# Partial sums of the fourth dense tile of a PEER layer leave PSUM every fourth block in place of every second

## The chip, the cores and the metric

The kernel runs on one core of a Trainium2 chip. The metric is the device time of one execution in microseconds (us), lower is better. Three runs of the kernel before gave 4597.64, 4600.57 and 4611.91 us; their median, 4600.57 us, is the time that a prediction is set against.

## The reference, cut to what matters

The program is a two-layer backbone over 256 context tokens and 512 latent tokens of width 1024. Each layer is a mixer (RWKV-7 heads and a Fourier transform in layer 0, attention and a convolution in layer 1) followed by a PEER layer, a product-key mixture of 16384 one-row experts. Only the PEER layer is touched:

```python
def chunk(tc):
    ...                                    # product keys: 16 experts per head and token, with a gate
    act = jax.nn.gelu(jnp.einsum("thkd,td->thk", pu[expert], tc), approximate=False) * gate
    return jnp.einsum("thk,thkd->td", act, pv[expert])
```

## The kernel before, in words

A PEER layer is computed in two ways side by side. **Dense tiles** (128 tokens each) are multiplied with all experts: the 16384 experts are 128 blocks of 128, and for a block `up_part` forms the activations of all dense tiles (matmuls of `proj`, line 392, into PSUM tile `pS`, then a Gelu on ScalarE, line 1237). They are multiplied by a table of gates that is zero for experts not chosen (line 1307, VectorE), and the products are contracted with the block's rows of `pv` (line 1291). **Gathered tiles** fetch their chosen rows of `pu` and `pv` one by one with an indirect DMA issued on GpSimd (line 1132), and VectorE reduces each row (lines 1137 and 1146). The fetches have three row buffers.

In layer 0 the four latent tiles are dense (`nd == 4`), and the two context tiles are gathered at the same time. In layer 1 three tiles are dense and one is gathered, and the lines that the change edits take the same values as before.

Every matmul runs three times, on high and low parts of its operands: `split` casts to the high part on ScalarE (line 379) and subtracts on VectorE for the low part (line 382). For block `it` of the down stage that gives four tiles, `ahi`, `alo` (activations) and `vhi`, `vlo` (rows of `pv`), the *part* of that block. They come from pools `act` and `pv`.

PSUM has eight banks. The sums of dense tiles 0 to 2 stay in six of them over all 128 blocks (`acc00` to `acc21`), and `pS` takes one. The fourth tile's sums, two halves of 512 columns, share the one that is left: PSUM tile `acc4` is filled from the last two parts for half 0, added to an SBUF tile of the same name by VectorE (line 1324; the very first time a ScalarE copy, line 1322), and then filled for half 1. So in every second block there are two groups of six matmuls (line 1320), and each may begin only when VectorE has emptied the bank after the group before. Four buffers of each part are there.

The order on each engine is set when the program is built, by a scheduler that plays the program through on its own timing; engines then run their lists strictly in order. `pace` hands out the gather steps over the blocks, so VectorE's list mixes casts, gate products, gather steps and the additions of line 1324. After the last block come the epilogue (lines 1352 and 1353, written out at line 1356) and the mixer of layer 1, which loads the two context tiles again (`nx`, line 207).

Of the kernel before, what the change touches and what calls it, by code (L numbers as in the profile page):

```python
# [17 lines left out]
PS = bass.MemoryType.PSUM  # L18
# [176 lines left out]
class Net:  # L195
# [1007 lines left out]
    def peer(self, l, dense, gath, xin, xout, front, done=None):  # L1203
# [5 lines left out]
        nd = len(dense)  # L1209
        n = nd * 128  # L1210
        with ExitStack() as st:
# [21 lines left out]
            def up_part(b, out, pS):  # L1233
                *u, i = self.wtile(up, self.I[f"l{l}_pu"][b], e_lo=V, q=nc.sync)
                p = pS.tile([128, 512], F32, name="pS")[:, :n]
                self.proj([(p, 0, n)], u, h)
                nc.scalar.activation(out=out, in_=p, func=AF.Gelu)  # L1237
                return i
            def pace(ins, w):
                nonlocal work  # L1240
                self.gstep(math.ceil(self.gleft * w / max(work, w, 1e-9)) if w else 0, ins)
                work -= w
            with ExitStack() as s2:
                sp, gp = self.tp(s2, "sel", 1), self.tp(s2, "gbig", 3)
                pp, pt = self.tp(s2, "gps", 3, space=PS), self.tp(s2, "gtp", 2, space=PS)
                pS = self.tp(s2, "pS", 2, space=PS)
# [14 lines left out]
            self.cs.close()  # L1261

            n3 = min(nd, 3)
            keep = 2 if nd == 4 else 1
            xp = self.tp(st, "act", 2 * keep)
            with ExitStack() as s2:
                pS = self.tp(s2, "pS", 3 - keep, space=PS)
                po = self.tp(s2, "acc", 1, space=PS)
                vw, gp = self.tp(s2, "pv", 2 * keep), self.tp(s2, "gl", 2)
                if nd == 4:  # L1270
                    acc4 = kp.tile([128, D], F32, name="acc4")
                parts = []
                acc = [[po.tile([128, 512], F32, name=f"acc{t}{hf}") for hf in range(2)] for t in range(n3)]

                pairs = sorted([((i + 0.5) / (NB // 2), 2 * i) for i in range(NB // 2)] +
                               [((i + 0.5 - OF) / (64 - NB // 2), NB + 2 * i) for i in range(64 - NB // 2)])
                order = [b + i for _, b in pairs for i in range(2)]
                fresh = [b for b in order if b >= NB]
                def go():
                    if fresh:  # L1280
                        b = fresh.pop(0)
                        ahead[b] = ap.tile([128, n], F32, name="a32f", bufs=2)
                        up_part(b, ahead[b], pS)
                ahead = {}
                go()
                def add(t, it, p):
                    ahi, alo, vhi, vlo = p
                    q = slice(t * 128, (t + 1) * 128)
                    for x, y, s, z in ((ahi, vhi, it == 0, False), (ahi, vlo, False, False), (alo, vhi, False, it == 127)):
                        for h2 in range(2):  # L1290
                            nc.tensor.matmul(acc[t][h2], x[:, q], y[:, h2 * 512:(h2 + 1) * 512], start=s, stop=z)  # L1291
                for it, b in enumerate(order):
                    if b % 2 == 0:
                        gt = gp.tile([128, 2 * nd, 2, 64], F32, name="gt")
                        nc.sync.dma_start(gt, gd[:, :, b:b + 2].rearrange("h p b t -> p h b t"))
                    vr = vw.tile([128, D], F32, name="vraw", bufs=2)
                    nc.sync.dma_start(vr, self.I[f"l{l}_pv"][b * 128:(b + 1) * 128])
                    vhi = vw.tile([128, D], F32R, name="vhi")
                    vlo = vw.tile([128, D], F32R, name="vlo")
                    self.split(vr, vhi, vlo)  # L1300
                    if b < NB:
                        a32 = ap.tile([128, n], F32, name="a32")
                        nc.sync.dma_start(a32, ad[b])
                    else:
                        a32 = ahead.pop(b)
                        go()
                    last = V.tensor_tensor(out=a32.rearrange("p (h t) -> p h t", t=64), in0=a32.rearrange("p (h t) -> p h t", t=64),  # L1307
                                           in1=gt[:, :, b % 2], op=OP.mult)
                    ahi = xp.tile([128, n], F32R, name="ahi")
                    alo = xp.tile([128, n], F32R, name="alo")  # L1310
                    self.split(a32, ahi, alo)
                    parts.append((ahi, alo, vhi, vlo))
                    four = nd == 4 and it % 2
                    for hf in range(2):
                        if four:
                            c = slice(hf * 512, (hf + 1) * 512)
                            p = po.tile([128, 512], F32, name="acc4")
                            for i, (xh, xl, yh, yl) in enumerate(parts):
                                for x, y, s, z in ((xh, yh, i == 0, False), (xh, yl, False, False), (xl, yh, False, i == 1)):
                                    nc.tensor.matmul(p, x[:, 384:512], y[:, c], start=s, stop=z)  # L1320
                            if it == 1:
                                nc.scalar.copy(out=acc4[:, c], in_=p)
                            else:
                                V.tensor_tensor(out=acc4[:, c], in0=p, in1=acc4[:, c], op=OP.add)
                        if it < 126 and hf == 0:
                            for t in range(n3):
                                add(t, it, parts[-1])
                    if it == 127:

                        for t in range(n3):  # L1330
                            for i in range(2):
                                add(t, 126 + i, parts[i - 2])
                    if four or nd < 4:
                        parts = parts[-1:] if nd < 4 else []
                    pace(last, W1 if b < NB else 2)
                self.gstep(self.gleft)
                if done:

                    done[0].close()
                    sp = self.tp(done[1], "ep", 2, side="right")  # L1340
                else:
                    sp = self.tp(s2, "ep", 2)
                xs = []
                for t in dense:
                    xs.append(sp.tile([128, D], F32, name="ex", bufs=nd))
                    self.load(xs[-1], xin[t])
                for i in ((3, 0, 1, 2) if nd == 4 else range(nd)):
                    x = xs[i]
                    for hf in range(2):
                        c = slice(hf * 512, (hf + 1) * 512)  # L1350
                        m = sp.tile([128, 512], F32, name="em")
                        V.tensor_tensor(out=m, in0=acc[i][hf] if i < 3 else acc4[:, c], in1=gr[:, c], op=OP.mult)
                        V.tensor_tensor(out=x[:, c], in0=x[:, c], in1=m, op=OP.add)
                    if l == 1:
                        self.final(x, sp)
                    nc.sync.dma_start(xout[dense[i]], x)
# [268 lines left out]
```

## Time and profile before

| what | value |
|---|---|
| median of three runs | 4600.57 us |
| the profiled execution's own time | 4596.4 us |
| its span on the core | 4594.3 us |
| TensorE matmul, busy | 4165.1 us (91%), 26113 matmuls |
| TensorE weight load, busy | 3437.0 us (75%) |
| VectorE, busy | 3539.4 us (77%) |
| ScalarE, busy | 1738.3 us (38%) |
| GpSimd, busy | 1614.0 us (35%) |
| mean granted TensorE clock | 0.945 |

The down stage of layer 0 lies between 1813 and 2922 us of the span (from the first matmul of line 1291 to the last of line 1320). Matmuls are pipelined: one is listed with some 0.39 us, and the next starts sooner than that, so that the number of matmuls in a stretch says more than the busy share. "PE" is TensorE's matmul, "PEld" its weight load, DVE is VectorE, ACT ScalarE, POOL GpSimd and SP the engine that issues most DMAs.

### The profile page before, as it was taken

To read this page: it belongs to the slowest core of one execution; us is meant where nothing else is said; L and a number is where in the kernel's file an instruction comes from. 1 tells how busy PE (TensorE), PEld (TensorE's weight loads), DVE (VectorE), ACT (ScalarE), POOL (GpSimd) and SP (SyncE) were. 2 spreads that over 40 slices of the span, in tenths; PEclk is the share of its full clock that TensorE was granted. 3 is DMA by queue.
4 is the path that set the end of the run, shared out by engine and by line. 5 is a ranking of instruction groups with operands and counts; after the bars stand their busy time and mean duration, and the time that the engine had idled before them with its cause. 6 is when DMAs were issued, how large, how long until landed. Compare 5 with 4: busy or idle time off the path is not lost. (4 is left out here: it accounts for less than half of the span.)

```text
span 4594.3 us, 69774 instructions
## 1 busy us (share of the span) xinstructions
PE 4165.1 (91%) x26113; PEld 3437.0 (75%) x26113; DVE 3539.4 (77%) x6647; ACT 1738.3 (38%) x2847; POOL 1614.0 (35%) x1146
## 2 busy tenths in 40 slices
PE   7998899984777998999999999879999979999998
PEld 5775668872656887777778888666789968888887
DVE  2676667798898997888787887685489968788875
ACT  3443123332213665222222222336437733333333
POOL 1432212315642231444444444383220034444430
PEclk9998899995888999999999999989999989999999
DMA  4344884336777788889898988411236599999994
GB/s 170 92 108 102 264 297 125 119 106 203 228 236 234 271 309 293 302 309 320 295 320 309 309 304 290 145 32 33 71 105 215 217 345 336 340 330 339 344 333 145
DMA packets 487280, 1062.00 MB, mean 231 GB/s; under 512 B 95095, under 2 KB 265847, under 8 KB 477207
## 3 DMA queue, kind: packets, MB, share of 16 engines
q1 hardware_dynamic: 371740, 594.02, 39.2%
q0 software_dynamic: 110592, 402.70, 25.2%
q10 hardware_dynamic: 4608, 60.82, 3.3%
q8 instruction: 206, 3.38, 0.3%
q14 instruction: 134, 1.09, 0.1%
HBM read 927.83 MB, written 129.56 MB: 230 GB/s over the span
## 5 line engine op out<-in xcount | busy, mean ns | idle before, releaser
L1132 POOL DMA_INDIRECT row<-in_l_pv_dram,gi x384 | 563.3, 1467 | 837.0 <-DVE rows L1146 706.3
L1132 POOL DMA_INDIRECT row<-in_l_pur_dram,gi x384 | 490.3, 1277 | 953.8 <-DVE ga L1137 532.6
L392 PE MATMUL pS<-h2hi,whi 128*128 128x512 f32 (+1 forms) x2048 | 757.0, 370 | 35.3 <-ACT a L1237 29.6
L392 PE MATMUL pS<-h2hi,wlo 128*128 128x512 f32 (+1 forms) x2048 | 754.7, 369 | 7.8 <-DVE wlo L382 7.8
L392 PE MATMUL pS<-h2lo,whi 128*128 128x512 f32 (+1 forms) x2048 | 753.4, 368 | 0.0
L1137 DVE CUSTOM_DVE_ANT_0 row<-row,rows 128x1024 f32<-128x1024 f32 x384 | 498.7, 1305 | 185.0 <-DMA row<-in_l_pur_dram,gi 183.0
L379 ACT CAST whi<-wraw 128x1024 fp32r<-128x1024 f32 x327 | 344.3, 1054 | 759.4 <-PE pS L392 554.9
L1146 DVE SCALAR_TENSOR_TENSOR rows<-row,ga,rows 128x1024 f32<-128x1024 f32 x381 | 488.5, 1282 | 148.5 <-DMA row<-in_l_pv_dram,gi 146.3
L1291 PE MATMUL acc<-vhi,ahi 128*128 128x512 f32 x1536 | 469.7, 392 | 14.8 <-ACT ahi L379 14.8
L1291 PE MATMUL acc<-vlo,ahi 128*128 128x512 f32 x1536 | 479.6, 391 | 0.8 <-DVE vlo L382 0.8
L1291 PE MATMUL acc<-vhi,alo 128*128 128x512 f32 x1536 | 471.3, 391 | 1.5 <-DVE alo L382 1.4
L392 PEld LDWEIGHTS pS<-h2hi,whi 128*128 128x128 f32 x2048 | 391.0, 191 | 83.4 <-ACT a L1237 31.8
L392 PEld LDWEIGHTS pS<-h2hi,wlo 128*128 128x128 f32 x2048 | 390.3, 191 | 50.9 <-DVE wlo L382 9.2
L392 PEld LDWEIGHTS pS<-h2lo,whi 128*128 128x128 f32 x2048 | 390.4, 191 | 43.8
L382 DVE TENSOR_TENSOR wlo<-wraw,whi 128x1024 fp32r<-128x1024 f32 x266 | 324.3, 1220 | 71.0 <-ACT whi L379 70.9
L379 ACT CAST vhi<-vraw 128x1024 fp32r<-128x1024 f32 x256 | 264.8, 1050 | 206.7 <-PE acc L1291 117.7
L1291 PEld LDWEIGHTS acc<-vhi,ahi 128*128 128x128 f32 x1536 | 288.3, 189 | 69.2 <-ACT ahi L379 15.2
L382 DVE TENSOR_TENSOR vlo<-vraw,vhi 128x1024 fp32r<-128x1024 f32 x256 | 309.8, 1221 | 37.1 <-ACT vhi L379 36.9
L1291 PEld LDWEIGHTS acc<-vlo,ahi 128*128 128x128 f32 x1536 | 289.4, 189 | 63.0 <-DVE vlo L382 1.5
L1291 PEld LDWEIGHTS acc<-vhi,alo 128*128 128x128 f32 x1536 | 288.9, 188 | 63.7 <-DVE alo L382 2.8
L379 ACT CAST ahi<-a32f 128x384 fp32r<-128x384 f32 (+1 forms) x148 | 83.3, 563 | 570.2 <-DVE a32f L1307 274.0
L1120 ACT ACTIVATE gbig<-gps 128x256 f32<-128x256 f32 x448 | 232.4, 670 | 112.1 <-PE gps L1118 86.8
(460 smaller groups left out, 7950.0 us busy)
## 6 DMA issues: line engine op xcount, KB each, us to landing
wraw<-in_l_pu_dram SPq DMA_DIRECT2D x256, 512.0 KB
vraw<-in_l_pv_dram SPq DMA_DIRECT2D x256, 512.0 KB
gd<-gbig ACTq DMA_DIRECT2D x28, 2048.0 KB
mw<-in_l_mod_w_dram SPq DMA_DIRECT2D x48, 1024.0 KB
gt<-gd SPq DMA_DIRECT2D x64, 512.0 KB
wraw<-in_l_pq_dram SPq DMA_DIRECT2D x48, 512.0 KB
gt<-gd SPq DMA_DIRECT2D x64, 384.0 KB
ab<-arb SPq DMA_DIRECT2D x24, 768.0 KB
```

The source lines that it names most:

```text
L379: e.copy(out=hi, in_=src)
L382: return (e_lo or nc.vector).tensor_tensor(out=lo, in0=src, in1=hi.bitcast(F32), op=OP.subtract)
L392: nc.tensor.matmul(ps, a[:, k, :], b[:, k, t0:t0 + n], start=s, stop=e)
L1120: nc.scalar.mul(out=g[:, :, t0 - h0:t0 - h0 + 4].rearrange("p e t -> p t e"), in_=p[:, :, i * 64:i * 64 + 64], mul=1.0 / GSC)
L1132: nc.gpsimd.indirect_dma_start(out=r, out_offset=None, in_=self.I[f"l{l}_{src}"], in_offset=bass.IndirectOffsetOnAxis(ap=idx[:, s:s + 1], ...
L1137: V.tensor_tensor_reduce(out=r, in0=r, in1=acc, scale=1.0, scalar=0.0, op0=OP.mult, op1=OP.add, accum_out=act[:, s:s + 1])
L1146: V.scalar_tensor_tensor(out=acc, in0=r, scalar=act[:, s:s + 1], in1=acc, op0=OP.mult, op1=OP.add)
L1291: nc.tensor.matmul(acc[t][h2], x[:, q], y[:, h2 * 512:(h2 + 1) * 512], start=s, stop=z)
```

## The change

The fourth tile's groups are formed in every fourth block, from the last four parts: twelve matmuls per group instead of six, half as many groups, and so half as many additions from PSUM into SBUF (62 of line 1324 where there were 126; the two copies of line 1322 remain). A part has to live up to four blocks now, so each of `ahi`, `alo`, `vhi` and `vlo` gets six buffers instead of four. These take 24 KB more of each partition. The buffers of `pS` (one with four dense tiles, two otherwise) and all of layer 1 keep their numbers.

```diff
-            keep = 2 if nd == 4 else 1
-            xp = self.tp(st, "act", 2 * keep)
+            xp = self.tp(st, "act", 6 if nd == 4 else 2)
             with ExitStack() as s2:
-                pS = self.tp(s2, "pS", 3 - keep, space=PS)
+                pS = self.tp(s2, "pS", 1 if nd == 4 else 2, space=PS)
                 po = self.tp(s2, "acc", 1, space=PS)
-                vw, gp = self.tp(s2, "pv", 2 * keep), self.tp(s2, "gl", 2)
+                vw, gp = self.tp(s2, "pv", 6 if nd == 4 else 2), self.tp(s2, "gl", 2)
...
-                    four = nd == 4 and it % 2
+                    four = nd == 4 and it % 4 == 3
...
-                                for x, y, s, z in ((xh, yh, i == 0, False), (xh, yl, False, False), (xl, yh, False, i == 1)):
+                                for x, y, s, z in ((xh, yh, i == 0, False), (xh, yl, False, False), (xl, yh, False, i == 3)):
...
-                            if it == 1:
+                            if it == 3:
```

With one line less, line 1291 becomes 1290, 1320 becomes 1319, 1324 becomes 1323, and so on. The scheduler orders the whole stage anew. TensorE's list has the same matmuls. A group of the second half of the columns, early in the stage, before and then with the change (each row writes `acc4` from one part; the number behind a name counts buffers handed out):

```order
L1291 MATMUL acc01_17629<-vlo_18409,ahi_18415 128x512
L1320 MATMUL acc4_18344<-vhi_18199,ahi_18237 128x512
L1320 MATMUL acc4_18344<-vlo_18200,ahi_18237 128x512
L1320 MATMUL acc4_18344<-vhi_18199,alo_18238 128x512
L1320 MATMUL acc4_18344<-vhi_18276,ahi_18314 128x512
L1320 MATMUL acc4_18344<-vlo_18277,ahi_18314 128x512
L1320 MATMUL acc4_18344<-vhi_18276,alo_18315 128x512
L1291 MATMUL acc00_17628<-vhi_18408,alo_18416 128x512
```

```order
L1319 MATMUL acc4_18427<-vhi_18191,ahi_18229 128x512
L1319 MATMUL acc4_18427<-vlo_18192,ahi_18229 128x512
L1319 MATMUL acc4_18427<-vhi_18191,alo_18230 128x512
L1319 MATMUL acc4_18427<-vhi_18268,ahi_18306 128x512
L1319 MATMUL acc4_18427<-vlo_18269,ahi_18306 128x512
L1319 MATMUL acc4_18427<-vhi_18268,alo_18307 128x512
L1319 MATMUL acc4_18427<-vhi_18347,ahi_18354 128x512
L1319 MATMUL acc4_18427<-vlo_18348,ahi_18354 128x512
L1319 MATMUL acc4_18427<-vhi_18347,alo_18355 128x512
L1319 MATMUL acc4_18427<-vhi_18384,ahi_18391 128x512
L1319 MATMUL acc4_18427<-vlo_18385,ahi_18391 128x512
L1319 MATMUL acc4_18427<-vhi_18384,alo_18392 128x512
```

Two groups of six become one of twelve. In the list before, 16 to 42 other matmuls stand between the end of a group and the start of the next (none before the very last group). With the change 23 to 37 stand there in 48 of the 63 places and 68 to 73 in the other 15.

On VectorE, from the addition of one half to that of the other, early in the stage (`rows` is the gathered tile's sum, one row of it per gather step; `acc` stands for `acc4`), before and then with the change:

```order
L1324 TENSOR_TENSOR acc_17627<-acc_18318,acc_17627 128x512
L1307 TENSOR_TENSOR a_18639<-a_18639,gt 128x512
L1307 TENSOR_TENSOR a_18676<-a_18676,gt 128x512
L1146 SCALAR_TENSOR_TENSOR rows_6122<-row,ga_7655,rows_6122 128x1024 x3
L382 TENSOR_TENSOR alo<-a32f,ahi 128x512
L1324 TENSOR_TENSOR acc_17627<-acc_18344,acc_17627 128x512
```

```order
L1323 TENSOR_TENSOR acc_17627<-acc_18395,acc_17627 128x512
L1146 SCALAR_TENSOR_TENSOR rows_6122<-row,ga_7655,rows_6122 128x1024 x3
L382 TENSOR_TENSOR vlo<-vraw,vhi 128x1024
L1146 SCALAR_TENSOR_TENSOR rows_6122<-row,ga_7655,rows_6122 128x1024
L1323 TENSOR_TENSOR acc_17627<-acc_18427,acc_17627 128x512
```

The gather steps, 350 in the stage in both, stand among the rest much as they did: 32 times three or more of them follow each other before, 31 times with the change. In 20 of the 31 batches the second addition stands right behind a `vlo`, in 3 of all 126 additions before.

On the queue of SP, where layer 0 ends and the mixer of layer 1 begins (`x_5_101` is the epilogue's first tile written out, `nx` the reloaded context tiles), before and then with the change:

```order
L207 DMA dw<-in_dw_w_dram 128x62
L207 DMA nx<-x_0_96 128x1024
L207 DMA nx<-x_1_97 128x1024
L1356 DMA x_5_101<-ex 128x1024
L1356 DMA x_3_99<-ex 128x1024
```

```order
L207 DMA dw<-in_dw_w_dram 128x62
L1355 DMA x_5_101<-ex 128x1024
L207 DMA nx<-x_0_96 128x1024
L207 DMA nx<-x_1_97 128x1024
L1355 DMA x_3_99<-ex 128x1024
```

The two loads moved behind the first write of the epilogue. In layer 1 rows of all engines but GpSimd change places here and there; what is computed there is the same.

## Rows read from the trace of the kernel before

**Rows 1.** Busy time by stretch: from:to, us, engines, granted clock, DMA share, GB/s.

```profile
1813.00:2922.00 1109.00, 1073.12 (x4637) 872.71 (x4635) 882.00 (x1060) 299.66 (x393) 469.35 (x349) 0.99 0.88 302
1900.00:2500.00 600.00, 567.69 (x2415) 456.56 (x2414) 478.67 (x631) 156.72 (x204) 260.55 (x200) 0.98 0.89 309
2500.00:2900.00 400.00, 399.29 (x1759) 329.53 (x1758) 321.66 (x340) 110.60 (x145) 165.80 (x121) 1.00 0.87 295
2600.00:2700.00 100.00, 100.00 (x443) 82.81 (x442) 80.08 (x85) 29.73 (x39) 44.20 (x31) 1.00 0.90 306
```

**Rows 2.** TensorE's waits, 1900 to 2500: us in total, times, longest.

```profile
PE acc L1320 <- DVE acc L1324: 28.3, 24, 2.7
PE acc L1320 <- DVE alo L382: 2.4, 2, 1.2
...
PEld acc L1320 <- DVE acc L1324: 41.3, 33, 3.1
```

**Rows 3.** VectorE's waits, 1900 to 2500, the longest in total.

```profile
DVE row L1137 <- DMA row<-in_l_pur_dram,gi: 73.4, 53, 3.8
DVE rows L1146 <- DMA row<-in_l_pv_dram,gi: 36.6, 26, 4.2
```

**Rows 4.** VectorE by line, 1900 to 2500: count, busy us, mean ns, idle before.

```profile
L1137 DVE CUSTOM_DVE_ANT_0 row<-row,rows 128x1024 f32<-128x1024 f32 x128 | 155.2, 1222 | 73.9 <-DMA row<-in_l_pur_dram,gi 73.4 <-issue 0.2
L1146 DVE SCALAR_TENSOR_TENSOR rows<-row,ga,rows 128x1024 f32<-128x1024 f32 x72 | 92.4, 1284 | 37.1 <-DMA row<-in_l_pv_dram,gi 36.6
L1324 DVE TENSOR_TENSOR acc<-acc,acc 128x512 f32<-128x512 f32 x66 | 45.2, 684 | 0.0
```

**Rows 5.** Timeline of VectorE: start, us, instruction, idle before it and what ended it.

```profile
2208.10 1.23 DVE L1137 CUSTOM_DVE_ANT_0 row<-row,rows 128x1024 f32<-128x1024 f32 x1 [3.76 <-DMA row<-in_l_pur_dram,gi]
...
2209.76 1.23 DVE L1137 CUSTOM_DVE_ANT_0 row<-row,rows 128x1024 f32<-128x1024 f32 x1 [0.42 <-DMA row<-in_l_pur_dram,gi]
...
2210.91 0.69 DVE L382 TENSOR_TENSOR alo<-a32f,ahi 128x512 fp32r<-128x512 f32 x1
2211.51 0.69 DVE L1324 TENSOR_TENSOR acc<-acc,acc 128x512 f32<-128x512 f32 x1
```

**Rows 6.** TensorE at the same place: its timeline, then the stretch that follows.

```profile
2209.16 0.39 PE L392 MATMUL pS<-h2hi,whi 128*128 128x512 f32 x1
2212.25 0.50 PE L1320 MATMUL acc<-vhi,ahi 128*128 128x512 f32 x1 [2.71 <-DVE acc L1324]
...
2212.00:2218.00 6.00, 5.75 (x18) 4.59 (x19) 6.00 (x10) 0.18 (x1) 3.06 (x3) 0.72 0.90 300
```

**Rows 7.** GpSimd's longest waits, 1900 to 2500.

```profile
POOL row L1132 <- DVE ga L1137: 198.8, 101, 4.7
POOL row L1132 <- DVE rows L1146: 105.5, 52, 7.8
```

**Rows 8.** Timeline at the stage's end: SP, ACT, DVE and PE.

```profile
2900.18 0.93 SPq L207 DMA_DIRECT2D nx<-x  x2
2924.09 7.77 SPq L1356 DMA_DIRECT2D x<-ex  x4
...
2906.78 1.06 ACT L310 ACTIVATE nj<-nx 128x1024 f32<-128x1024 f32 x1 [6.48 <-DMA nx<-x]
...
2909.76 0.75 DVE L314 TENSOR_SCALAR nj<-nx,ns 128x1024 f32<-128x1024 f32 x1
2921.45 0.69 DVE L1324 TENSOR_TENSOR acc<-acc,acc 128x512 f32<-128x512 f32 x1 [0.30 <-PE acc L1320]
2930.83 0.69 DVE L1353 TENSOR_TENSOR ex<-ex,em 128x512 f32<-128x512 f32 x1
...
2919.75 0.50 PE L1320 MATMUL acc<-vhi,ahi 128*128 128x512 f32 x1 [0.78 <-DVE acc L1324]
```

**Rows 9.** Layer 1's PEER stage: its stretch, and TensorE's longest wait, 3700 to 4594.

```profile
3800.00:4500.00 700.00, 699.46 (x3421) 621.64 (x3420) 563.60 (x699) 249.45 (x340) 308.40 (x222) 1.00 0.95 336
...
PE acc L1291 <- ACT ahi L379: 14.8, 1, 14.8
```

## The prediction

> **What bounds the kernel now.** I first asked which part of the program the change can reach at all: the down stage of layer 0, 1813 to 2922 us, which has every matmul of line 1320. The table of stretches comes first. Where TensorE waits for nothing it starts 443 matmuls in 100 us, one per 0.2257 us [rows 1]. At that pace the 2415 matmuls between 1900 and 2500 us need 545 us and take 600: 55 us are lost. The 1759 matmuls between 2500 and 2900 need 397 us and take 400. So nearly all that can be won in this stage lies in those 600 us.
>
> The list of TensorE's waits says what ends them. 24 times the engine stood idle until line 1324 had emptied `acc4`, 28.3 us in all; the weight loads, which come a step earlier, met the same wait 33 times [rows 2]. Idle time counts from the end of a 0.39 us matmul, though the next could have started 0.226 us after its start, so each wait costs 0.16 us more: 28.3 + 24 x 0.16 = 32 us. The granted clock is the second loss. In the 6 us after one such wait it is 0.72 on average, the lower level (1.2 GHz) for part of them, after 2.71 us of idling [rows 6]; over the 600 us it is 0.98 [rows 1], which is 600 x 0.02 = 12 us. Together 44 of the 55 us hang on the additions; the rest is small waits for `alo` and what I can't assign.
>
> Then I asked why the additions are late. VectorE's waits in the same stretch are for gathered rows: 73.4 and 36.6 us [rows 3], 110 of the 121 us in which it idles (600 less 478.7 [rows 1]). None of its long waits is for TensorE. The timeline shows it in one place: VectorE waits 3.76 us for a row, reduces it and another, does an `alo`, and only then the addition, and TensorE starts 2.71 us late [rows 5, 6]. GpSimd in turn waits for VectorE to give a row buffer back [rows 7]. So here **VectorE's list, with the fetches it waits for, is the slower chain**, and TensorE meets it at line 1324.
>
> **The change part by part.** *Half the additions go.* 66 of them stand in the stretch, 0.684 us each [rows 4]; 33 remain, and 33 x 0.684 = 22.6 us leave VectorE's list. I work out what that is worth in two ways.
>
> From TensorE: 66 meetings become 33, and 7 of these have 68 or more matmuls (15 us at 0.2257) between the groups, against waits of at most 3.1 us [rows 2] that came with at most 42 (9.5 us); those can't wait. 26 of 66 remain, so 44 x 40/66 = 27 us are saved, if VectorE's list gets shorter by as much.
>
> From VectorE: since its list is the slower chain, the stretch gets shorter by what leaves it, 22.6 us, less what its waits for rows grow by. Where the row behind a removed addition is late anyway, VectorE only waits longer. 79 of the stretch's 200 gather steps wait (53 + 26 [rows 3], 128 + 72 [rows 4]); if the addition ahead of every such step were lost in its wait, 40% of 22.6 would go and 13.6 us be left. But most of a fetch's cycle starts when VectorE hands a buffer back [rows 7], so a step that comes earlier also fetches earlier, and the gather steps stand in runs of the same length as before. I take 21 us, close to the upper end, and keep 13.6 and 27 as bounds.
>
> The Trainium skill (Perfetto Trace Analysis, Identifying the Most-Contended Engine) judges TensorE by the busy share of its weight loads rather than of its matmuls, and other engines by occupancy. By that rule VectorE is the more contended in the stretch (80% against 76%) and TensorE in the next (82% against 80%) [rows 1], which agrees with where the loss is; by matmul busy share (95%) TensorE would be it in both, and the sum would be TensorE's 27 us.
>
> *The rest of the stage.* Between 2500 and 2900 us TensorE runs at its pace [rows 1]; additions that go there free VectorE and buy nothing. TensorE's matmuls are the same in number and shape. The four-part group starts as late as its last part, as the two-part group did.
>
> *Two more buffers of each part* take a cause of waiting away and add none: a part lives longer, but when a group ends four buffers come free and two parts are still ready, as before. What it could cost is bunching, since four casts become possible at once; that is a rival below. Zero, while the casts hide beneath the 36 matmuls of line 1291 (8 us) that two ready blocks give TensorE.
>
> *The end of the stage.* Before, the last addition comes after the last matmul, and TensorE waits 0.78 us just ahead of that [rows 8]. Now 13 matmuls follow the last group, 2.9 us, which cover a 0.69 us addition. Gain 1.5 us.
>
> *The reloads of the context tiles* move behind the epilogue's first write on SP, which waits for VectorE's epilogue. Before, they were issued at 2900.18, ScalarE began with them at 2906.78 and VectorE scaled the first at 2909.76 [rows 8], all beneath the last matmuls. Now they go out where the write did, at 2924.1 or 1.5 earlier. With the same 6.6 and 3.0 us the first is ready at about 2932, the epilogue on VectorE ends at 2931.5 (2930.83 + 0.69 [rows 8]), and two scalings (0.75 us each) with their reciprocals come on top. With the queue emptier than before the load may be faster; with the writes of the other tiles in its way, slower. Loss 2.5 us, 0 to 6.
>
> *Layer 1* does the same work in a slightly different order. From 3800 to 4500 us TensorE never stops there (3421 matmuls, clock 1.00); its one long wait is 14.8 us [rows 9]. I take 0, and half that wait, 7 us, either way as bounds.
>
> Sum against the profiled execution's own 4596.4 us: -21 - 1.5 + 2.5 + 0 = -20, 4576.4 us. The median of the runs is 4.2 us above that execution, so I forecast 4600.6 - 20 = 4580.6 us.
>
> **The rivals.**
>
> *A, TensorE comes close to its pace.* If the additions are also what holds the gather back (GpSimd waits for VectorE 304 us of the stretch [rows 7]), rows come earlier, and most of the 55 us return, say 40: 4600.6 - 40 = 4560. For it: TensorE and VectorE each wait for the other's chain now, so a shorter one helps twice. Against: VectorE's list would have to get 40 us shorter, 17 more than leave it.
>
> *B, the rows take it.* VectorE waits for rows as much longer as it has less to do. The fetches run beside matmul operands on a DMA that is 0.89 busy [rows 1], and a faster stage asks for more. Then 5 us or so remain: 4596.
>
> *C, bunched casts, and slower.* In 20 of 31 batches the second addition stands right behind a `vlo`, whose buffer the group before it has to free, and ScalarE must cast ahead of it. If that holds VectorE up once per batch ahead of a gather step, GpSimd gets its buffer late and the next row waits as well: 73.4/53 = 1.4 us per wait [rows 3], times 32 batches is 45 us, against 22.6 saved: +22, 4623. It decides from 0.7 us per batch (22.6/32). Against: 23 to 37 matmuls, 5.2 us and more, lie between two groups, and rows are bunched as before.
>
> *D, given back in layer 1.* The stage gains, and another wait like the one of 14.8 us [rows 9] arises in layer 1's new order: 4595.
>
> **How the numbers follow.** Chances: the forecast 0.50 (its own range 4566 to 4594, from the bounds 13.6 and 27 and the two ends of the smaller terms), A 0.15, B 0.18, C 0.09, D 0.08. A measurement of this kernel can tell about 0.3%, 13.8 us, from no change: faster means below 4586.8, slower above 4614.4. Of the forecast 0.45 lies below and 0.05 within; with A faster is 0.60. The rest of the forecast, B and D make 0.31 within, and C 0.09 slower. The range runs from 4556 (A and a little beyond) to 4603 (past B and D); C and the far side of A are left out.
>
> **What the trace of the changed kernel would show.** Right: 62 additions of 0.68 us; the idle time that they end on TensorE down from 28.3 us to some 12 between 1900 and 2500 (that is, in the blocks that stood there), with a higher granted clock; VectorE's waits for rows about as long as now; the stage some 21 us shorter; the first matmul of layer 1's projections 1 us later after the last one of the stage. Wrong: waits for rows that grow by 10 us or more (B); TensorE waiting as long as now with half the additions, or for `vlo` and `alo` (C); a stage of under 1075 us (A); a layer 1 whose length changes by more than 7 us (D). My argument fails as a whole if VectorE turns out to wait for TensorE in the stretch, since then its list was not the slower chain.

## The result and the profile after

The changed kernel is slower. Four runs of it gave 4655.74, 4638.55, 4656.03 and 4659.77 us, median 4655.89; four runs of the kernel before on the same chip gave a median of 4599.10. The ratio is 1.0104, with a 95% interval of 1.0083 to 1.0124, so some 48 us by the ratio and 57 by the medians. Forecast were 4580.6 us, faster than before, and a range of 4556 to 4603; the time lies 53 us above that range.

The profiled execution took 4655.74 us, its span 4654.0, its mean granted clock 0.939 (0.945 before). Lines of the changed kernel are numbered one lower than before: 1290 for 1291, 1319 for 1320, 1323 for 1324. The down stage of layer 0 now lies between 1816 and 2979 us. Its table of stretches (columns as in [rows 1]: stretch, its length, the busy time of TensorE matmul, weight load, VectorE, ScalarE and GpSimd with counts, granted clock, DMA share, GB/s):

```profile
1816.00:2979.00 1163.00, 1086.99 (x4636) 881.78 (x4634) 845.45 (x995) 297.22 (x385) 445.73 (x349) 0.98 0.84 287
1900.00:2500.00 600.00, 550.18 (x2317) 442.80 (x2316) 441.82 (x574) 151.00 (x195) 250.65 (x194) 0.97 0.86 297
2500.00:2900.00 400.00, 380.10 (x1642) 310.67 (x1641) 288.98 (x298) 105.69 (x137) 134.40 (x116) 0.98 0.85 282
```

Against [rows 1] the stage is 54 us longer with the same matmuls, and VectorE has 37 us less to do in it (845 against 882). The loss is in both parts: 98 matmuls fewer between 1900 and 2500 us (22 us at 0.2257 us each), and 117 fewer (26 us) between 2500 and 2900, where TensorE had run at its pace. The program ahead of the stage took 3 us longer. What follows the stage took 1675.0 us (4654.0 less 2979), against 1672.3 before.

The waits of the whole stage (total us, times, longest):

```profile
ACT vhi L379 <- DMA vraw<-in_l_pv_dram: 259.4, 56, 11.6
...
ACT vhi L379 <- PE acc L1319: 130.2, 15, 12.4
DVE rows L1146 <- DMA row<-in_l_pv_dram,gi: 127.3, 83, 3.9
...
DVE row L1137 <- DMA row<-in_l_pur_dram,gi: 85.5, 55, 3.8
DVE vlo L382 <- ACT vhi L379: 56.0, 23, 6.7
...
PE acc L1319 <- DVE acc L1323: 40.5, 18, 5.6
...
PE pS L392 <- ACT a32f L1237: 15.5, 6, 4.0
...
PE acc L1290 <- ACT ahi L379: 7.6, 5, 2.1
PE acc L1319 <- ACT ahi L379: 7.5, 3, 4.0
```

The same list before:

```profile
DVE rows L1146 <- DMA row<-in_l_pv_dram,gi: 97.2, 72, 4.6
...
PE acc L1320 <- DVE acc L1324: 31.1, 27, 2.7
...
ACT vhi L379 <- DMA vraw<-in_l_pv_dram: 10.4, 7, 3.0
```

The first line stands out. `vraw` is the buffer into which a block's rows of `pv` are loaded; ScalarE casts it to `vhi`, VectorE subtracts for `vlo`, and then the buffer is free. There are two of them, in both kernels. ScalarE waited for them 10.4 us before and 259.4 us after. VectorE never waited for `vhi` before; now it does so 23 times. Its waits for rows grew from 170.6 us (73.4 of [rows 3] and 97.2) to 212.8. TensorE's meetings with the addition became fewer (18 in place of 27) and longer.

On TensorE two waits are new, both for work of ScalarE: 15.5 us until the Gelu of line 1237 has emptied `pS`, and 15.1 us for `ahi`. One of them, by the timelines of ScalarE and TensorE:

```profile
2545.85 2.00 ACT L379 CAST vhi<-vraw 128x1024 fp32r<-128x1024 f32 x2 [8.23 <-PE acc L1319]
2558.01 1.04 ACT L379 CAST vhi<-vraw 128x1024 fp32r<-128x1024 f32 x1 [10.16 <-DMA vraw<-in_l_pv_dram]
...
2559.90 0.59 ACT L1237 ACTIVATE a32f<-pS 128x512 f32<-128x512 f32 x1
...
2560.54 0.79 PE L392 MATMUL pS<-h2hi,whi 128*128 128x512 f32 x1 [3.84 <-ACT a32f L1237]
```

ScalarE stood 10.16 us for a raw block, the Gelu behind it in its list came late (no idle time stands ahead of it), and TensorE stood 3.84 us for the Gelu. Over the stage TensorE's idle time grew from 36 us (1109 less 1073.1) to 76 (1163 less 1087.0), and its granted clock fell from 0.99 to 0.98, an estimated 12 us more (1163 x 0.02 less 1109 x 0.01); together that is about the 54 us.

One batch of four, by ScalarE's timeline (start, duration, instruction, idle before it and what ended it):

```profile
2219.46 2.00 ACT L379 CAST vhi<-vraw 128x1024 fp32r<-128x1024 f32 x2
2229.36 1.05 ACT L379 CAST vhi<-vraw 128x1024 fp32r<-128x1024 f32 x1 [7.90 <-DMA vraw<-in_l_pv_dram]
2231.90 1.05 ACT L379 CAST vhi<-vraw 128x1024 fp32r<-128x1024 f32 x1 [1.50 <-DMA vraw<-in_l_pv_dram]
```

and by SP's, which issues the loads:

```profile
2196.25 2.13 SPq L1296 DMA_DIRECT2D vraw<-in_l_pv_dram  x2
...
2224.13 12.09 SPq L1296 DMA_DIRECT2D vraw<-in_l_pv_dram  x4
```

Two raw blocks had been asked for at 2196 and lay ready until TensorE's second group, from 2217.17 on, read four parts for the last time and freed them within 3 us:

```profile
2217.17 0.50 PE L1319 MATMUL acc<-vhi,ahi 128*128 128x512 f32 x1 [2.52 <-DVE acc L1323]
...
2219.79 0.39 PE L1319 MATMUL acc<-vhi,alo 128*128 128x512 f32 x1
```

Two casts followed directly. The third block could be asked for only at 2224.13, when the first `vlo` had given a raw buffer back, and ScalarE stood for 7.90 us. The group itself had begun 2.52 us late, behind the addition of the first half.

### The profile page after: what moved, and what is told of

The parts are those of the page before. It is cut to its first block, busy times and chain, and to the rows that moved or that the text cites. A ratio compares the mean times of both kernels' runs of the same rounds, so it can differ in the third digit from the quotient of the medians.

```text
span 4654.0 us, 69618 instructions
## 1 busy us (share of the span) xinstructions
PE 4186.2 (90%) x26113; PEld 3451.8 (74%) x26113; DVE 3498.6 (75%) x6583; ACT 1739.2 (37%) x2847; POOL 1593.1 (34%) x1146
## 5 line engine op out<-in xcount | busy, mean ns | idle before, releaser
L1132 POOL DMA_INDIRECT row<-in_l_pv_dram,gi x384 | 536.3, 1397 | 902.8 <-DVE rows L1146 765.7
```

The costliest lines, as they stand in the source:

```text
L1132: nc.gpsimd.indirect_dma_start(out=r, out_offset=None, in_=self.I[f"l{l}_{src}"], in_offset=bass.IndirectOffsetOnAxis(ap=idx[:, s:s + 1], ...
```

## The experiments

The comparisons are ratios to the kernel before, run beside each kernel on the same chip. Two causes were suspected: the raw buffers, for the loss, and the rows, for the gain that didn't come.

### More raw buffers

```diff
-                    vr = vw.tile([128, D], F32, name="vraw", bufs=2)
+                    vr = vw.tile([128, D], F32, name="vraw", bufs=3)
```

The second run has 4 there, and `bufs=5` for `alo`.

> The changed kernel with three buffers of the raw value block (vraw) in place of two. Theory R (raw ring): four part buffers come free together, four casts want four raw blocks, two buffers hold two, and the third load is issued only after the first second-part subtraction; ScalarE's wait for raw blocks, 259 us in the stage of the changed kernel against 10 before, falls to between 100 and 180 us, and the time to 4605 to 4635. Rival H (parts held): four of six part buffers are held until the group, and two ahead are too few whatever feeds them: the time stays within 10 us of 4656, and ScalarE's wait only moves from raw blocks to part buffers. Rival S (the second half's group waits for the first half's addition, which has one accumulator between them): the time stays within 10 us of 4656 and TensorE's waits of 40.5 us for additions stay.

> The changed kernel with four buffers of the raw value block; for their space one of the six buffers of the activations' second part (alo) is given up. Theory R: as many raw blocks wait as parts come free: ScalarE's wait for raw blocks falls below 80 us in the stage, VectorE's waits for casts (56 us) below 20, and the time to 4570 to 4605. Rival H: within 10 us of 4656 or above it, since one buffer fewer makes it worse. Rival S: within 10 us of 4656.

Three raw buffers gave 1.0045 (1.0028 to 1.0062), four 1.0038 (1.0025 to 1.0052): 27 and 30 of the 48 us. ScalarE's waits for raw blocks fell from 259.4 to 184.5 us with three, and to 5.3 with four. So the third buffer gave nearly all of the gain with most of these waits left: their sum is no measure of what they cost. With four, ScalarE casts four blocks without a pause (timeline, same columns):

```profile
2209.82 3.89 ACT L379 CAST vhi<-vraw 128x1024 fp32r<-128x1024 f32 x4
```

Waits in the stage with four raw buffers:

```profile
DVE rows L1146 <- DMA row<-in_l_pv_dram,gi: 141.3, 78, 7.2
...
DVE row L1137 <- DMA row<-in_l_pur_dram,gi: 84.5, 60, 4.0
...
PE acc L1290 <- DVE alo L382: 20.8, 12, 3.1
PE acc L1319 <- DVE acc L1323: 19.8, 11, 4.3
...
PE acc L1290 <- ACT ahi L379: 13.3, 6, 3.5
...
DVE vlo L382 <- ACT vhi L379: 6.0, 3, 3.3
ACT vhi L379 <- DMA vraw<-in_l_pv_dram: 5.3, 4, 2.8
```

The wait for raw blocks is gone, and that for additions, 19.8 us against 31.1 before, is nearly what the prediction wanted. But VectorE's waits for rows rose further, to 225.8 us, and TensorE now waits for `alo` and `ahi`. So the raw buffers are a large part of the loss, but theory R had expected too much of them (4570 to 4605 us with four, and waits of 100 to 180 us with three): the time stays above that of before. Rivals H and S, which had it at 4656, fall as main causes. Four raw buffers were paid for with one of `alo`; the control has that buffer missing and two raw buffers:

> The changed kernel with five buffers of the activations' second part in place of six and two raw buffers, the control for the run with four raw buffers (1.0038), which had paid for its space with that buffer. If the missing buffer is what was left of the loss there: 1.018 or more. If it costs nothing: 1.007 to 1.014, that of the changed kernel.

It gave 1.0077 (1.0054 to 1.0100), so the missing buffer costs nothing that can be measured. Against this control four raw buffers are worth 0.4%, 18 of 35 us; with the 27 of 48 for three, that is half to 60% of the loss. TensorE waits 26.9 us for `alo` there too (2.2 in the changed kernel), and less for additions (27.6 against 40.5): that wait comes with the five buffers, and takes the place of another. ScalarE's waits for raw blocks were 268.2 us, as in the changed kernel.

### Six buffers alone, and parts freed in twos

The second run is the kernel before with `6 if nd == 4 else 2` buffers of each part:

> The kernel before with the six buffers of each part alone; the sums still go to SBUF every second block. Theory R: two parts come free at a time and two raw buffers feed them, so the time is that of before within 14 us (4585 to 4613). Rival H: four parts ahead in place of two give TensorE's waits for second parts back: 4575 to 4590. A rival P, by which the larger rings or their place in SBUF cost the time by themselves: 4640 to 4660.

0.9999 (0.9984 to 1.0015). Bigger rings by themselves neither cost nor gain. ScalarE's waits for raw blocks are 22.0 us there, with two raw buffers and parts freed in twos. The third run takes the changed kernel and staggers its halves:

```diff
-                    four = nd == 4 and it % 4 == 3
+                    four = nd == 4 and it % 2
...
-                        if four:
+                        if four and (it % 4 == 1 + 2 * hf or it == 127):
...
+                            used = parts[-2:] if hf == 0 and it in (1, 127) else parts[-4:]
...
-                        parts = parts[-1:] if nd < 4 else []
+                        parts = parts[-1:] if nd < 4 else parts[-2:]
```

> The changed kernel with its two halves taken apart: the first half's group of the last four blocks stands behind every fourth block from the second on, the second half's behind every fourth from the fourth on, so that parts come free in twos, and still up to four are held; the number of additions is that of the changed kernel (one more at the end). Theory R: 4565 to 4595, ScalarE's wait for raw blocks below 60 us, since two raw buffers again suffice. Rival H: 4635 to 4660, since four of six are held as often. Rival S: the wait between the halves is gone (TensorE's waits for additions below 20 us), so 4580 to 4615, but ScalarE's wait for raw blocks stays where it was.

0.9946 (0.9929 to 0.9962): 25 us faster than before, and 73 faster than the changed kernel, with one addition more than that and with as many parts held. Two things differ: parts come free two at a time, and the two halves' groups don't follow each other on the bank. A run in the last section of the experiments prices the second by itself, 0.45%, where parts come free in twos with and without it; no run has the halves apart and parts freed in fours, so how the 73 us divide between the two is not shown. The staggered kernel's waits in the stage:

```profile
DVE rows L1146 <- DMA row<-in_l_pv_dram,gi: 104.5, 81, 3.5
DVE row L1137 <- DMA row<-in_l_pur_dram,gi: 82.4, 53, 4.3
...
ACT vhi L379 <- DMA vraw<-in_l_pv_dram: 28.1, 15, 7.9
...
PE acc L1320 <- DVE acc L1324: 18.5, 10, 4.2
```

ScalarE waits 28.1 us for raw blocks with the same two buffers. So theory H (four of six held are too many) falls as the main cause. Three runs on its remainder:

> The changed kernel with four raw buffers and five buffers of each part in place of six: four are still held until the group and four still come free at once, but one block in place of two is ready beyond them. Theory B (bunching: what is left of the loss with four raw buffers, 1.0038 of before, is four casts and four subtractions in a row on VectorE's list): 1.002 to 1.008. Theory H (too few parts ahead of TensorE): one block fewer ahead costs more than the raw ring did, 1.012 to 1.030.

> The staggered halves (parts free in twos, up to four held) with five buffers of each part in place of six. Theory B: parts come in twos with one to three blocks ahead, so within 0.3% of the staggered kernel with six (0.992 to 0.998 of before). Theory H: 1.000 to 1.015, since with four held only one buffer is ahead.

> The staggered halves with three raw buffers. Theory: with parts freed in twos two raw buffers suffice, and ScalarE's 28 us of waits for raw blocks cover nothing that TensorE waits for: within 0.3% of the staggered kernel with two (0.992 to 0.998 of before). If raw blocks still held the stage up there: 0.986 to 0.991.

Five buffers seem to cost 0.3% in both: 1.0065 (1.0047 to 1.0084) against 1.0038 in fours, 0.9974 (0.9960 to 0.9989) against 0.9946 in twos. Both lie within what theory B allowed and far from H's 1.012 and more. A third raw buffer changes nothing in twos: 0.9948 (0.9931 to 0.9966). Two suffice there.

The Trainium skill (Trainium Kernel Development and Optimization, Best Practices) advises to double-buffer so that transfers overlap with compute. The traces agree where parts come free in twos (28.1 us of waits for raw blocks with two buffers, and no gain from a third) and not where they come free in fours (259.4 us): there two is too few.

### What the additions are worth

The kernel before, without its additions:

```diff
-                            else:
+                            elif it == 127:
                                 V.tensor_tensor(out=acc4[:, c], in0=p, in1=acc4[:, c], op=OP.add)
```

> The kernel before without 124 of its 126 VectorE additions of the fourth tile's sums (the last block's two stay): the fourth tile's output then holds only the first and the last pair of blocks, and nothing else changes. It prices the prediction's own term by itself. If 62 additions fewer are worth 21 us, as the prediction had it, 124 fewer are worth about 42: 0.990 to 0.992 of before. If the additions' waits only change their name (TensorE then waits for the next thing of VectorE's list), 0.996 to 1.000. If an addition costs more than its 0.68 us and its wait (it also holds up the casts behind it), under 0.988.

0.9985 (0.9968 to 1.0001): 7 us for 124 additions of 0.684 us. But ScalarE waited 264.5 us for raw blocks here too, since the new order again put four casts close together. So the raw buffers could have eaten the gain. Two more runs take that away:

> The kernel before without 124 of the 126 additions (the fourth tile's output then holds only the first and last pair of blocks) and with four raw buffers. Without the additions alone the time was 0.9985 of before, and ScalarE waited 264 us for raw blocks, as in the changed kernel. Theory A (an addition is worth what the prediction said, and the raw ring took it back there): 0.986 to 0.994. Theory G (rows set VectorE's pace and take whatever leaves its list): 0.996 to 1.001, with waits for rows of 220 us or more.

> The kernel before with four raw buffers alone, the control for the run without additions: ScalarE waited 10 us for raw blocks in the stage of before, so 0.997 to 1.003. If more raw loads in flight slow the row fetches: 1.003 to 1.010.

The control is 1.0002 (0.9982 to 1.0022); without the additions it is 0.9972 (0.9951 to 0.9992). That is 0.3%, some 13 us, for 124 additions (9 to 20 us, an estimate from the ten times of each). The control's stage in the table of stretches, and its waits for rows:

```profile
1811.20:2933.10 1121.90, 1073.58 (x4633) 872.31 (x4631) 879.03 (x1053) 297.46 (x391) 473.38 (x348) 0.99 0.86 298
```

```profile
DVE rows L1146 <- DMA row<-in_l_pv_dram,gi: 101.7, 71, 5.8
DVE row L1137 <- DMA row<-in_l_pur_dram,gi: 80.3, 59, 4.0
```

The same two views of the kernel without additions:

```profile
1814.70:2919.60 1104.90, 1069.61 (x4633) 873.80 (x4631) 803.40 (x929) 297.65 (x391) 474.24 (x348) 0.99 0.87 302
```

```profile
DVE rows L1146 <- DMA row<-in_l_pv_dram,gi: 161.6, 80, 6.3
...
DVE row L1137 <- DMA row<-in_l_pur_dram,gi: 100.8, 70, 4.2
...
PE acc L1320 <- ACT ahi L379: 26.2, 13, 6.4
```

75.6 us left VectorE's busy time (879.0 to 803.4), and its waits for rows grew by 80.4 us (182.0 to 262.4); the stage became 17 us shorter in these two profiles. TensorE, which no longer waits for an addition, waits 26.2 us for `ahi` in its place. This is what the prediction's rival B had, as an outcome. B's reason, a DMA that is too busy, is another matter, and the next runs test it.

### More rows in flight

The gathers have three row buffers (`RB`). A fourth lets GpSimd ask one step earlier:

```diff
-RB = 3
+RB = 4
```

> The kernel before with four row buffers for the gathers in place of three (the constant RB, used by the gathers of the whole program), so that a row is asked for one step earlier. It tests whether VectorE's list is held by rows, 171 us of waits in the stage of before and 226 without the additions. Theory G (the rows set VectorE's pace, so that work taken off its list turns into waits for rows): the waits for rows fall below 80 us and the time to 0.985 to 0.996 of before. Theory T (VectorE's busy time and TensorE's needs set the pace, rows only fill gaps): waits for rows fall, the time stays at 0.997 to 1.003.

> The kernel before without 124 of the 126 additions (the fourth tile's output then holds only the first and last pair of blocks) and with four row buffers. Theory G: with rows at hand the additions have their price, so this is at least 0.5% below the kernel before with four row buffers alone, against 0.15% with three: 0.975 to 0.990 of before. Theory T: what the additions left is taken by another wait again, within 0.3% of before with four row buffers alone.

> The staggered halves (six buffers of each part, two raw buffers) with four row buffers. Theory G: 0.978 to 0.990 of before, below either change alone (0.9946 for the halves). Theory T: 0.991 to 0.998, that of the halves alone.

> The changed kernel with four row buffers. Theory G with the raw ring and the bunching as second causes: rows come earlier but four raw blocks are still wanted from two buffers, so 1.000 to 1.010 of before, against 1.0104 with three row buffers; ScalarE's wait for raw blocks stays above 180 us. If late rows were the whole cause of the loss: 0.990 to 0.999.

| kernel | three row buffers | four row buffers |
|---|---|---|
| before | 1 | 0.9852 (0.9831 to 0.9873) |
| changed | 1.0104 (1.0083 to 1.0124) | 0.9904 (0.9887 to 0.9922) |
| staggered halves | 0.9946 (0.9929 to 0.9962) | 0.9851 (0.9834 to 0.9869) |
| before, without additions | 0.9985 (0.9968 to 1.0001) | 0.9889 (0.9873 to 0.9906) |
| changed, three raw buffers | 1.0045 (1.0028 to 1.0062) | 0.9845 (0.9803 to 0.9887), with alo 5 |

One constant gives the kernel before 68 us (by the ratio; the two profiled executions differ by 49). Its stage in the table of stretches, and waits in it:

```profile
1820.90:2879.30 1058.40, 1056.44 (x4659) 873.91 (x4657) 877.01 (x1058) 300.23 (x394) 480.26 (x347) 1.00 0.90 315
```

```profile
DVE rows L1146 <- DMA row<-in_l_pv_dram,gi: 33.3, 26, 3.1
...
DVE row L1137 <- DMA row<-in_l_pur_dram,gi: 28.9, 26, 3.6
...
PE acc L1320 <- DVE acc L1324: 1.4, 2, 0.8
```

The stage is 50 us shorter than in [rows 1], the granted clock 1.00 throughout, and of TensorE's waits for additions 1.4 us are left, with all 126 additions in place. The additions were late because rows were late, not because there were many of them. Once rows are at hand the stage stands at TensorE's pace, and the staggered halves add nothing (0.9851). Leaving the additions out even costs there, against theory G's expectation: ScalarE waits 258.2 us for raw blocks in that run, so perhaps the raw buffers bind; no run without additions has four of both. The changed kernel gains more, 2.0%, and comes out below the 1.000 to 1.010 that was expected: about half of its loss shows only while rows are late. It stays 0.5% above the kernel before with four row buffers, with 179.1 us of waits for raw blocks. What is left lies late in the stage: between 1900 and 2500 us it starts 2649 matmuls, TensorE's pace, but between 2500 and 2850 only 1453, where the kernel before with four row buffers starts 1546 (21 us). One more run takes up that remainder, with four row, three raw and five `alo` buffers:

> The changed kernel with four row buffers, three raw buffers and five of the activations' second part. With four row buffers alone it was 0.9904, against 0.9852 for the kernel before with four row buffers. Theory R: the raw ring is half mended, so 0.985 to 0.989. If the casts in a row are all that is left, and not the raw blocks: 0.989 to 0.993.

0.9845 (0.9803 to 0.9887), just below theory R's range: by the times nothing of the loss is left. But the interval is wide, and the profile doesn't show a mended ring:

```profile
ACT vhi L379 <- DMA vraw<-in_l_pv_dram: 173.4, 22, 12.7
```

ScalarE waits for raw blocks nearly as long as with two of them (179.1 us). The profiled execution was the slowest of the four (4560.68 us), and its stage was still 13 us longer than that of the kernel before with four row buffers. That the third raw block takes the remainder is therefore not shown.

### Fewer additions, or halves that don't follow each other

The staggered kernel's 25 us don't fit with additions that are worth 13. Two runs tell the separation of the halves from the number of additions; the first forms each half's group in every second block (half 0 after odd blocks, half 1 after even ones), the second drops the additions of the staggered kernel, by the edit shown above for the kernel before. The first, against the staggered kernel:

```diff
-                    four = nd == 4 and it % 2
+                    four = nd == 4 and it > 0
...
-                        if four and (it % 4 == 1 + 2 * hf or it == 127):
+                        if four and (it % 2 != hf or it == 127):
...
-                            used = parts[-2:] if hf == 0 and it in (1, 127) else parts[-4:]
+                            used = parts[-2:] if it % 2 else parts[-3:-1]
...
-                            if it == 1 + 2 * hf:
+                            if it == 1 + hf:
...
-                        parts = parts[-1:] if nd < 4 else parts[-2:]
+                        parts = parts[-2:] if nd == 4 and it % 2 else parts[-1:]
```

> The halves apart as in the staggered kernel, six buffers of each part, but each half's group is formed in every second block from two parts (half 0 after odd blocks, half 1 after even ones), with as many additions as before (125 in place of 126). It asks which of the two, fewer additions or halves that don't follow each other, gave the staggered kernel its 0.9946. If the separation did: 0.992 to 0.997 of before. If the number of additions did: 0.998 to 1.003.

> The staggered halves without their VectorE additions but the last of each half (the fourth tile's output then lacks most of its blocks). If the additions that are left there still cost time as the 62 removed ones seemed to, 0.988 to 0.992 of before. If rows take what leaves VectorE's list, 0.993 to 0.998, with waits for rows 30 us or more above the 187 us of the staggered kernel.

With 126 additions, as many as before (the trace has 126, the expectation above counted 125), the separated halves give 0.9955 (0.9934 to 0.9976), where the six buffers alone gave 0.9999. Without additions the staggered kernel gives 0.9941 (0.9921 to 0.9960), against 0.9946 with its 63; its waits for rows grew by 26 us (186.9 to 212.9), a little less than the 30 that were expected. So the gain comes from the separation (rival S had the link, though as the cause of the loss). Taking 61 of the staggered kernel's 63 additions away can't be told from nothing; with four row buffers the staggered kernel with 63 and the kernel before with 126 take the same time.

By which wait the separation gains is not settled. The nearest control is the kernel before with six buffers of each part. TensorE's waits for additions there:

```profile
PE acc L1320 <- DVE acc L1324: 46.0, 28, 4.2
```

With the halves apart these are 30.5 us, and VectorE's waits for rows 160.0 us against 194.4 in that control. But the kernel before itself, which takes the same time as that control, has 31.1 and 170.6, and its stage was 1108 us long in its profile where the control's was 1121. One profile of each is too few to choose a wait by.

## Why the prediction was wrong

**The place was right.** Of the 60 us between the two spans 54 lie in the down stage of layer 0. What follows it changed by 2.7 us, where +1 was forecast; between profiles of kernels that take the same time that length differs by up to 6 us (1667 us with six buffers of each part alone, at 0.9999). Layer 1 keeps its pace (3424 matmuls between 3800 and 4500 us, against 3421 in [rows 9]). At the stage's end the last addition was covered, as forecast. The reloads of `nx` went out at 2979.10, after the epilogue's first write, and were the late work then, as forecast: ScalarE began with them at 2984.75. The first matmul of layer 1's projections started 33 us after the last one of the stage, against 30 before, where 1 us more was forecast.

**The failed step for the sign: "Two more buffers of each part take a cause of waiting away and add none".** The buffers by themselves are free (0.9999). What it overlooked is what fills them. In the kernel before, parts come free in twos and two raw buffers stand ready. In the changed one four come free together, and the third and fourth cast wait for loads that nothing covers (7.90 and 1.50 us in the batch shown). The Gelus and casts behind them in ScalarE's list come late, and TensorE waits for these (30.6 us, none before). The text looked at the casts' time, "beneath the 36 matmuls", and didn't ask where the third cast's operand is. The trace of before had the answer, in the waits of SP's queue over the stage:

```profile
SPq L1297 <- DVE vlo L382: 394.5, 124, 13.3
```

Line 1297 issues the raw loads, so nearly every one of the 128 was already issued only when a `vlo` gave a buffer back. The runs show what this costs. With three or four raw buffers half to 60% of the loss goes. With frees in twos two raw buffers are enough: at six buffers of each part the time is that of before. With staggered halves the loss is gone too, but there the halves are also apart. About half of the loss goes with a fourth row buffer; these shares overlap, since each is taken with the other shortage in place. Why 0.4% is left at four raw buffers and late rows was not isolated. Four casts are then followed by as many subtractions on a list that waits for rows (225.8 us), which is argued, not shown.

**Rival C was the right family, with the wrong link and a chance of 0.09.** It had "bunched casts" and a second addition behind a `vlo`. It priced 1.4 us per batch and put the point of decision at 0.7, with 4623 us as its time; measured were 4655.89. VectorE's waits for `vhi`, 56.0 us over 32 batches, are 1.75 us each, well past it. But its argument against, matmuls between the groups, spoke of TensorE's list; the shortage was in the loads.

**The failed step for the size: "the stretch gets shorter by what leaves it ... I take 21 us, close to the upper end".** This term is mis-sized. 124 additions, about twice the 64 that the change removes, are worth 13 us by the pair of runs with four raw buffers, so half of them 6 to 7, below the bound of 13.6. The ground given was that a gather step that comes earlier also fetches earlier. The runs show otherwise: with 75.6 us of work removed, VectorE waited 80.4 us longer for rows. A row took 6.1 us from issue to landing in the changed kernel (median of 128 issues of line 1132), and three buffers can't hide that behind steps of 1.22 us [rows 4], 3.7 us for three, unless other work stands between them. The additions were such work. The rows of before had shown it: 110 of 121 idle us were for rows [rows 3], and GpSimd waited for buffers [rows 7]. Both were read as VectorE being the slower chain, when the ring of three rows was: a fourth row buffer gave 0.9852. B, at a chance of 0.18, had this outcome, but for another reason, a DMA that is 0.89 busy; with four row buffers the DMA took 0.90 in the stage, and the waits for rows fell. B's own sign of "waits for rows that grow by 10 us or more" came in as 17.5 us between 1900 and 2500, while the work that left was 24 us (45.2 of [rows 4] to 21.2).

**TensorE's side of that term held in count, not in length.** Meetings with the addition in that stretch were to fall from 24 to some 10, and 12 us of idle time to be left:

```profile
PE acc L1319 <- DVE acc L1323: 25.2, 10, 5.4
```

They did fall to 10, but each lasted 2.5 us in place of 1.2, since VectorE's list came late to them all. The granted clock of the stretch, which was to rise, went from 0.98 to 0.97.

**"Between 2500 and 2900 us ... additions that go there free VectorE and buy nothing"** was silent on losses: 26 us were lost there. The bunched casts come in every batch, whether VectorE has time to spare or not; that they are the cause there is argued, and the raw blocks can't be all of it. With four raw buffers, where ScalarE's waits for them are gone, the same 400 us have 1618 matmuls, 32 us lost.

**A version that beats both:** the kernel before with four row buffers, 0.9852. With staggered halves it is the same within the intervals, and the halves alone are worth 0.5%.

## What to carry to other kernels

When a change makes a group of buffers come free together, count the buffers of every ring upstream, back to the DMA: the shallowest sets how many refills can start at once. Work taken off an in-order list is worth its time only if the list is not held by something that arrives at its own rate; if the idle time of an engine is nearly all one kind of DMA, first try one more buffer of that DMA. An addition that ends a stall need not be its cause: ask what the engine did ahead of it.

## What the runs showed of the hardware

The list of DMA issues between 1900 and 2500 us (tile, queue, count, median us from issue to landing) of the changed kernel, and of the changed kernel with four row buffers:

```profile
row<-in_l_pur_dram,gi POOLq DMA_INDIRECT x128, 6.1
row<-in_l_pv_dram,gi POOLq DMA_INDIRECT x66, 6.3
```

```profile
row<-in_l_pur_dram,gi POOLq DMA_INDIRECT x128, 7.0
row<-in_l_pv_dram,gi POOLq DMA_INDIRECT x86, 6.8
```

With a fourth row in flight each takes up to 0.9 us longer, and the waits for rows in the stage still fell from 212.8 to 74.6 us. The DMA engines, 0.84 busy in the changed kernel's stage, went to 0.89, and 0.88 to 0.90 in the kernel before: the transfers had room, only the requests were late. And where TensorE didn't wait, in the kernel before with four row buffers, its granted clock was 1.00 over all 1058 us, 2.4 GHz, at a matmul every 0.227 us (4659 of them), so that both losses of [rows 6], the idle time and the lower level after it, went together.
